# A four-branch encoder layer on one core: q and k by rows of three parts in DRAM, gating on chip, a third tile bank, the norm in 13 steps

## The chip, the cores and the metric
The kernel runs on one core of one Trainium2 chip. A core has TensorE (PE, matmuls into PSUM), VectorE (DVE), ScalarE (ACT) and GpSimd (POOL), and SyncE (SP), which here issues nearly all DMAs. Each engine works through its own instructions in order and waits on semaphores where a tile isn't ready. The metric is device time in microseconds, the median of several executions.

## What is computed
One layer on 1024 tokens with 1024 channels, all in float32:

```python
h = rmsnorm(x, norm_g[l])
z = h @ w_in[l]
qa, ka, va, glu_a, glu_b, pool_in, sgu_u, sgu_v, gates = jnp.split(z, split_at, axis=-1)
y_a = neighborhood_attention(qa, ka, va, na_rpb[l])
y_b = conformer_conv(glu_a, glu_b, conv_dw_w[l], conv_dw_b[l], conv_ln_g[l], conv_ln_b[l], conv_pw[l])
y_c = multiscale_pool(pool_in, pool_w[l], pool_scale[l])
y_d = spatial_gating(jax.nn.gelu(sgu_u), jax.nn.gelu(sgu_v), sgu_ln_g[l], sgu_ln_b[l], sgu_w[l], sgu_b[l])
y = jnp.concatenate([y_a, y_b, y_c, y_d], axis=-1) * jax.nn.silu(gates)
x = x + y @ w_out[l]
```

A last rmsnorm follows. Attention has 8 heads of 32 channels over windows of 8 x 16 tokens. The convolution branch is a depthwise convolution of 31 taps, a LayerNorm over its 256 channels (mean and variance over channels, so over partitions here), a swish and a 256 x 256 matmul. The spatial gating multiplies u by a mix of v over 128 positions.

## The kernel before
Matmuls take float32 split into a high and a low part, three products each (hi x hi, hi x lo, lo x hi).

**Column tiles.** `w_in` is worked through in 20 column tiles of 128 channels by 1024 tokens. `prep` loads a tile's weights (wraw) and splits them (whi, wlo). `gemm_bank` makes one half of a tile, 512 tokens, in one PSUM bank z_ps by 24 matmuls (L371), and an `evac_*` function takes it out. I number these 40 halves banks 0 to 39. The order of tiles is the list `work`: GLU gates and values (GB0, GA0, GB1, GA1), Q0, K0, pool (PO0, PO1), u (U0, U1), Q1, K1, and then the eight gate tiles G6, G7, G4, G5, G0, G2, G3, G1 (banks 24 to 39). Two PSUM banks are shared by all z_ps; the convolution has its own accumulator bank (ac), small matmuls another (b_ps), attention outputs another (pv), and scores two tiles (sa, sb).

**Work beside the column tiles.** After each bank the main loop takes pieces from three generators: attention (18 steps over banks 18 to 37), the convolution's 97 taps (over banks 4 to 22; most are DVE instructions, L584) and the convolution's norm (5 steps over banks 23 to 27). So the program's order is set by this count; a scheduler then places the instructions on each engine. Attention step j makes the scores of two heads for 256 queries (`att_scores`, L475 to L478, eight small matmuls), the exponent of step j-1 (`att_exp`, DVE L481 to L509 and ACT L500; M is a maximum, R a sum, rp on POOL a reduction over partitions) and, every second step, an output (`att_out`, L516 and L520). Steps 0 to 7 are head group 0 and 8 to 15 head group 1.

**Keys and queries.** `evac_q` and `evac_k` write hi and lo of a head group to DRAM (q_d, k_d, 128 partitions). `att_keys` loads a head's key tile kst: three loads of 32 partitions (hi, lo, hi) and one of 32 constant rows (kc_d). `att_loads` does the same for the queries (qst) and loads vk. All are issued on SP, in order.

**The norm.** `conv_norm` subtracts the mean (L612 makes it, L614 subtracts it), makes the variance (L622), sends it through DRAM in two hops (s_d, cr, sq) to spread it over partitions, scales (L637), applies the swish (L641 to L644) and makes the 256 x 256 matmul in yb (L651, L652).

**The gates.** `evac_u` makes u and, with `sgu` results, the gated u; it stores it to yd_d in DRAM. `evac_g` multiplies a branch by its gate: for tiles 6, 7 (spatial gating) and 4, 5 (pool) it loads the branch from DRAM into yr at its first half (L722), takes tanh (L725), multiplies z by yr (L727) and adds (L728). L730 and L731 do the same for branches that are in SBUF. After bank 39 the output GEMM begins (L822 on).

## Time and profile before
| | us |
|---|---|
| median of 3 runs | 436.57 (436.07 to 437.01) |
| the profiled execution | 435.86 |
| its span in the trace | 434.1 |
| PE busy | 415.9 (96%) |
| DVE busy | 312.3 (72%) |
| ACT busy | 184.8 (43%) |
| POOL busy | 112.2 (26%) |

PE is the engine that sets the time; its granted clock is at full speed but for one dip. A share of busy time is an average over the whole span: what a change is worth is read in the stretch where it acts, from the windows, the waits and the timeline of that stretch. A row of the timeline gives the start, the time from the first start to the last end of equal neighbours, the engine, the line, output <- input, the shape and the count, and in brackets the idle time before it with what ended it. Matmuls overlap, so the pitch from start to start tells more than the length of one.

### The profile page before, as it was taken

What the parts mean: (1) busy time and instruction counts of PE and PEld (TensorE: products, weight loads), DVE (VectorE), ACT (ScalarE), POOL (GpSimd) and SP (SyncE); (2) the same over time, 40 slices, a digit from 0 to 9 for tenths busy, and PEclk for the clock granted to TensorE, in tenths of its full rate; (3) what the DMA queues carried; (4) which work ended last, traced back from release to release, by engine and by line L of the source; (5) the groups of instructions that cost most, each with busy time, mean ns of one, the idle gap of its engine ahead of it and who ended that gap; (6) DMA issues with size and microseconds to landing.
All of it is one profiled execution on the core that took longest, in us unless ns stands there. A gap on an engine that the chain in (4) does not pass through costs nothing.

```text
span 434.1 us, 5888 instructions
## 1 busy us (share of the span) xinstructions
PE 415.9 (96%) x2150; PEld 331.2 (76%) x2150; DVE 312.3 (72%) x540; ACT 184.8 (43%) x314; POOL 112.2 (26%) x90
## 2 busy tenths in 40 slices
PE   7899999999999999999978889999999999999994
PEld 6788878888888778777846647787787788888883
DVE  4798676888988799999798647997882580093332
ACT  6757655222232328334336733344342452254332
POOL 0763402322226821111111101221111243620000
PEclk9999999999999999999995999999999999999998
DMA  7995106311775124163893141522011384402222
GB/s 273 421 418 186 54 25 206 88 48 51 228 245 150 48 97 146 50 219 104 271 235 90 52 168 54 170 94 65 11 48 61 122 269 183 145 2 97 97 98 97
DMA packets 28294, 59.56 MB, mean 137 GB/s; under 512 B 3910, under 2 KB 13354, under 8 KB 28266
## 3 DMA queue, kind: packets, MB, share of 16 engines
q1 hardware_dynamic: 28122, 58.93, 40.9%
q8 instruction: 17, 0.28, 0.3%
q10 hardware_dynamic: 144, 0.26, 0.2%
q14 instruction: 11, 0.09, 0.1%
HBM read 46.71 MB, written 12.47 MB: 136 GB/s over the span
## 4 chain that ended last, share of the span: by engine, by line
PE 80%; DMA 9%; DVE 5%; SPq 2%; ACT 1%; issue 1%; POOL 1%; DVEq 0%; ACTq 0%; POOLq 0%
PE z_ps L371 45%; DMA yr<-yd_d 3%; PE sb L213 3%; PE z_ps L213 3%; PE sb L822 3%; PE sb L856 3%; PE z_ps L822 2%; PE b_ps L856 2%; PE z_ps L856 2%; DMA xT_sb<-in_xT_dram 2%; PE pv L516 2%; PE sa L822 1%; PE ac L213 1%; PE b_ps L822 1%; PE pv L822 1%; PE ac L822 1%
## 5 line engine op out<-in xcount | busy, mean ns | idle before, releaser
L371 PE MATMUL z_ps<-hhi,whi 128*128 128x512 f32 x320 | 90.0, 400 | 1.5 <-DVE yr L728 1.3
L371 PE MATMUL z_ps<-hlo,whi 128*128 128x512 f32 x320 | 89.6, 398 | 0.0
L371 PE MATMUL z_ps<-hhi,wlo 128*128 128x512 f32 x320 | 87.8, 395 | 0.0
L371 PEld LDWEIGHTS z_ps<-hhi,whi 128*128 128x128 f32 x320 | 59.3, 190 | 17.8 <-issue 3.0
L371 PEld LDWEIGHTS z_ps<-hlo,whi 128*128 128x128 f32 x320 | 60.3, 189 | 14.8 <-issue 2.5
L371 PEld LDWEIGHTS z_ps<-hhi,wlo 128*128 128x128 f32 x320 | 60.5, 190 | 13.8 <-issue 1.1
L488 POOL PARTITION_ALL_REDUCE R<-M x16 | 29.9, 1868 | 134.3 <-DVE M L509 128.9
L584 DVE SCALAR_TENSOR_TENSOR ac<-d,pk,ac 128x512 f32<-128x512 f32 x62 | 46.6, 751 | 2.6 <-ACT ac L596 0.9
L360 POOL TENSOR_TENSOR wlo<-wraw,whi 128x256 fp32r<-128x256 f32 x36 | 27.4, 784 | 68.6 <-ACT whi L354 68.6
L354 ACT ACTIVATE whi<-wraw 128x512 fp32r<-128x512 f32 x40 | 25.0, 627 | 33.3 <-PE z_ps L371 31.5
L500 ACT ACTIVATE T<-T 128x1280 f32<-128x1280 f32 x16 | 20.4, 1272 | 15.5 <-DVE T L499 15.5
L584 DVE SCALAR_TENSOR_TENSOR ac<-ch,dws,ac 128x512 f32<-128x512 f32 x30 | 22.6, 755 | 1.8 <-ACT ac L585 0.8
L831 ACT ACTIVATE jk<-res 128x512 f32<-128x512 f32 (+1 forms) x17 | 10.2, 604 | 26.6 <-DVE res L829 25.6
L356 DVE TENSOR_TENSOR wlo<-wraw,whi 128x512 fp32r<-128x512 f32 x22 | 16.8, 764 | 5.1 <-ACT whi L354 5.0
L781 POOL TENSOR_TENSOR wlo<-wraw,whi 128x512 fp32r<-128x512 f32 x8 | 12.1, 1524 | 31.7 <-ACT whi L780 18.9
L829 DVE SCALAR_TENSOR_TENSOR res<-sa,res 128x512 f32<-128x512 f32 x2 | 1.4, 686 | 22.6 <-PE sa L822 22.6
L725 ACT ACTIVATE sg<-z_ps 128x512 f32<-128x512 f32 x16 | 9.5, 596 | 15.5 <-PE z_ps L371 14.1
L499 DVE TENSOR_TENSOR T<-T,pv 128x768 f32<-128x768 f32 x16 | 15.2, 948 | 0.0
L483 DVE SCALAR_TENSOR_TENSOR T<-sb,bt 128x768 f32<-128x768 f32 x16 | 15.2, 948 | 0.0
L505 DVE TENSOR_TENSOR R<-T 128x512 f32<-128x512 f32 x16 | 13.2, 827 | 2.6 <-ACT T L500 2.6
L481 DVE SCALAR_TENSOR_TENSOR T<-sa,bt 128x512 f32<-128x512 f32 x16 | 11.0, 685 | 3.7 <-PE pv L516 2.4
L781 POOL TENSOR_TENSOR wl<-wraw,wh 128x512 fp32r<-128x512 f32 x8 | 10.2, 1294 | 11.3 <-ACT wh L780 11.3
(279 smaller groups left out, 821.6 us busy)
## 6 DMA issues: line engine op xcount, KB each, us to landing
wraw<-in_w_in_dram SPq DMA_DIRECT2D x20, 512.0 KB
res<-in_x_dram SPq DMA_DIRECT2D x8, 512.0 KB
wraw<-in_w_out_dram SPq DMA_DIRECT2D x8, 512.0 KB
out_dram<-res SPq DMA_DIRECT2D x15, 256.0 KB
kst<-k_d SPq DMA_DIRECT2D x24, 136.0 KB
xT_sb<-in_xT_dram SPq DMA_DIRECT2D x6, 512.0 KB
qst<-q_d SPq DMA_DIRECT2D x24, 128.0 KB
vk<-va_d SPq DMA_DIRECT2D x8, 256.0 KB
```

The lines of the kernel that those rows point to most:

```text
L213: pe.matmul(z, lhsT=ha[:, 2 * c + k, ts], rhs=wa[:, k, :], start=(c == 0 and n == 0 and k == 0), stop=(c == 3 and n == 2 and k == 1))
L354: s.activation(out=hi, in_=raw[:, 4 * q:4 * q + 4], func=AF.Copy)
L356: v.tensor_tensor(out=lo, in0=raw[:, 4 * q:4 * q + 4], in1=hi, op=ALU.subtract)
L360: g.tensor_tensor(out=lo[:, w:w + 2], in0=raw[:, 4 * q + w:4 * q + w + 2], in1=hi[:, w:w + 2], op=ALU.subtract)
L371: pe.matmul(z, lhsT=wa[:, k, :], rhs=ha[:, 4 * q + k, b * 512:(b + 1) * 512], start=(n == 0), stop=(n == 3 * KO - 1))
L483: v.scalar_tensor_tensor(out=T[:, :, 256:640], in0=sb[:, :, 0:384], scalar=DH ** -0.5, in1=mf, op0=ALU.mult, op1=ALU.add)
L488: g.partition_all_reduce(R.rearrange("p h x -> p (h x)"), M.rearrange("p h x -> p (h x)"), P, bass.bass_isa.ReduceOp.max)
L500: s.activation(out=T, in_=T, func=AF.Exp)
L584: v.scalar_tensor_tensor(out=ac, in0=src, scalar=w, in1=ac, op0=ALU.mult, op1=ALU.add)
L781: g.tensor_tensor(out=lo[q], in0=raw[:, q], in1=hi[q], op=ALU.subtract)
L822: pe.matmul(acc[t], lhsT=y_[kt][:, ts], rhs=w_[q], start=(j == 0 and q == 0 and n == 0), stop=(j == 3 and q == 1 and n == 2))
L856: pe.matmul(o[:, c0:c1], lhsT=y_[kt][:, ts], rhs=w_[j][:, q, c0:c1], start=(j == 0 and q == 0 and n == 0), stop=(j == 3 and q == 1 and n = ...
```

## The change
Four parts.

- q_d and k_d hold, for each of 128 channels, a row of three parts (hi, hi, lo for q and hi, lo, hi for k). Three stores in place of two for each; a key tile is loaded by one DMA of 96 partitions, queries by one too. The key tiles are four fixed buffers (kst0 to kst3), so the constant rows are loaded for head group 0 only.
- The gated u stays in its SBUF tile (ut) and is tile 6 and 7's branch; yd_d, its two stores and two loads are gone. The pool branch's loads (yc_d) are issued two tiles ahead (`back`).
- Of the gate tiles' banks 24, 27, 30 and 33 go into the convolution's accumulator bank (ac), which gives three banks in turn.
- The convolution ends at bank 21, and the norm has 13 steps over banks 22 to 33 in place of 5 over 23 to 27. yb uses the tiles of sq.

```diff
-ATT0, ATT1, CONV0, CONV1 = 18, 37, 4, 22
+ATT0, ATT1, CONV0, CONV1, NORM1 = 18, 37, 4, 21, 33
...
     ya += [slot("ya") for _ in range(2)]
-    yr = {kt: slot("yr") for kt in (6, 7, 4, 5)}
+    yr = {kt: slot("yr") for kt in (4, 5)}
     sq = [slot("sq") for _ in range(2)]
-    yb = [slot("yb") for _ in range(2)]
+    yb = sq
 
...
-        z = zbank()
+
+        z = pso.tile([P, 512], F32, name="ac") if CONV1 < bank < ATT1 - 1 and bank % 3 == 0 else zbank()
...
-    k_d = dram.tile([2, 2, 4, DH, SW], F32, name="k_d")
+
+    q_d = dram.tile([2, P, 3, S], F32, name="q_d")
+    k_d = dram.tile([2, P, 3, SW], F32, name="k_d")
...
-                for n, src in enumerate((hi, lo)):
-                    ld.dma_start(out=q_d[hg, n].rearrange("h d x -> (h d) x"), in_=src[:, 0:S].bitcast(F32))
+                for n, src in enumerate((hi, hi, lo)):
+                    ld.dma_start(out=q_d[hg, :, n], in_=src[:, 0:S].bitcast(F32))
...
-                for n, src in enumerate((hi, lo)):
-                    ld.dma_start(out=k_d[hg, n].rearrange("h d x -> (h d) x"), in_=src.bitcast(F32))
+                for n, src in enumerate((hi, lo, hi)):
+                    ld.dma_start(out=k_d[hg, :, n], in_=src.bitcast(F32))
...
 
+
+    kbuf = {}
+
+    def ktile(h):
+        if h not in kbuf:
+            kbuf[h] = at.tile([P, SW], F32R, name=f"kst{h}", bufs=1)
+        return kbuf[h]
+
     def att_loads(gi):
         hg, b = groups[gi]
         vk[gi] = at.tile([P, 4, P], F32, name="vk")
@@ -433,20 +443,18 @@
                                              ap=[[GW, P], [256 * GW, 4], [1, P]]))
         qst[gi] = at.tile([P, 4, 256], F32R, name="qst")
 
-        for n in range(2):
-            src = q_d[hg, n, :, :, b * 256:(b + 1) * 256]
-            for c in range(2 - n):
-                o = 64 * n + 32 * c
-                ld.dma_start(out=qst[gi][o:o + 32].bitcast(F32), in_=src.rearrange("h d x -> d h x"))
+        src = q_d[hg, 0:DH, 0, b * 256:(b + 1) * 256]
+        ld.dma_start(out=qst[gi][0:96].bitcast(F32),
+                     in_=bass.AP(tensor=src.tensor, offset=src.offset, ap=[[S, 96], [96 * S, 4], [1, 256]]))
         ld.dma_start(out=qst[gi][96:128].rearrange("p h x -> p (h x)").bitcast(F32), in_=qm_d[32 * b:32 * b + 32])
 
     def att_keys(hg, h):
-        kst[hg, h] = at.tile([P, SW], F32R, name="kst", bufs=4)
-
-
-        for c, n in enumerate((0, 1, 0)):
-            ld.dma_start(out=kst[hg, h][32 * c:32 * c + 32].bitcast(F32), in_=k_d[hg, n, h])
-        ld.dma_start(out=kst[hg, h][96:128].bitcast(F32), in_=kc_d)
+
+        kst[hg, h] = ktile(h)
+        ld.dma_start(out=kst[hg, h][0:96].bitcast(F32),
+                     in_=k_d[hg, DH * h:DH * h + DH].rearrange("d n x -> (d n) x"))
+        if hg == 0:
+            ld.dma_start(out=kst[hg, h][96:128].bitcast(F32), in_=kc_d)
 
...
+            yield
...
+        yield
         for c in range(2):
             v.tensor_tensor(out=cc[c][:, 0:S], in0=cc[c][:, 0:S], in1=rb, op=ALU.mult)
+            s.activation(out=cc[c][:, 0:S], in_=cc[c][:, 0:S], func=AF.Identity, scale=cvec[:, 1, c:c + 1],
+                         bias=cvec[:, 2, c:c + 1])
+            yield
 
         for c in range(2):
             t = sq[c][:, 0:S]
-            s.activation(out=cc[c][:, 0:S], in_=cc[c][:, 0:S], func=AF.Identity, scale=cvec[:, 1, c:c + 1],
-                         bias=cvec[:, 2, c:c + 1])
             s.activation(out=t, in_=cc[c][:, 0:S], func=AF.Tanh, scale=0.5)
             v.scalar_tensor_tensor(out=cc[c][:, 0:S], in0=t, scalar=1.0, in1=cc[c][:, 0:S], op0=ALU.add, op1=ALU.mult)
-        yield
+            yield
         for c in range(2):
             for b in range(2):
-                sl = slice(b * 512, (b + 1) * 512)
                 ps = bbank()
                 for k in range(2):
-                    pe.matmul(ps, lhsT=pw[:, k, c * P:(c + 1) * P], rhs=cc[k][:, sl], start=(k == 0), stop=(k == 1))
+                    pe.matmul(ps, lhsT=pw[:, k, c * P:(c + 1) * P], rhs=cc[k][:, b * 512:(b + 1) * 512], start=(k == 0),
+                              stop=(k == 1))
                 s.activation(out=yb[c][:, 0:S].rearrange("p (n e) -> p n e", e=2)[:, :, b], in_=ps, func=AF.Copy, scale=0.5)
-            yield
-
-
-    yd_d = dram.tile([2, P, S], F32, name="yd_d")
+                yield
+
 
     def evac_u(c):
...
-            if b == 1:
-                ld.dma_start(out=yd_d[c], in_=u[:, 0:S])
...
 
-    y = {0: ya[0], 1: ya[1], 2: yb[0], 3: yb[1]}
+    y = {0: ya[0], 1: ya[1], 2: yb[0], 3: yb[1], 6: ut[0], 7: ut[1]}
     y.update(yr)
 
-    def evac_g(kt, src):
+    def evac_g(kt, early):
         def f(b, z):
             br = y[kt]
             sl = slice(b * 512, (b + 1) * 512)
-            if b == 0 and src is not None:
-                ld.dma_start(out=br[:, 0:S], in_=src)
 
             sg = at.tile([P, 512], F32, name="sg")
             s.activation(out=sg, in_=z, func=AF.Tanh, scale=0.5)
-            if src is not None:
...
-    work += [(T_G + kt, evac_g(kt, src)) for kt, src in
-             ((6, yd_d[0]), (7, yd_d[1]), (4, yc_d[0]), (5, yc_d[1]), (0, None), (2, None), (3, None), (1, None))]
+    work += [(T_G + kt, evac_g(kt, n < 4)) for n, kt in enumerate((6, 7, 4, 5, 0, 2, 3, 1))]
+
+    back = {T_G + kt: (yr[kt], yc_d[kt - 4]) for kt in (4, 5)}
 
...
+        if n + 2 < len(work) and work[n + 2][0] in back:
+            dst, src = back[work[n + 2][0]]
+            ld.dma_start(out=dst[:, 0:S], in_=src)
 
         for b in ((1, 0) if n == 0 else (0, 1)):
             evac(b, gemm_bank(ct, b))
             bank += 1
             if bank == 2:
                 bias_rows()
...
                 if b0 <= bank:
                     for _ in range(done(bank, count, b0, b1) - done(bank - 1, count, b0, b1)):
```

What that does to the instructions' order, at three places. Lines of after are 1 to 11 higher: L372 is the column-tile matmul, L483 to L486 the scores, L524 and L528 the output, L732/L733 and L735/L736 the gates' products.

SP, before, the loads for head group 1 (key tiles by parts of 32 partitions, then queries, then the spatial gating's load):

```order
L526 DMA o_d<-sg 4x256
L448 DMA kst<-k_d 32x1088 x4
L449 DMA kst<-kc_d 32x1088
L349 DMA wraw<-in_w_in_dram 128x1024
L448 DMA kst<-k_d 32x1088 x3
L449 DMA kst<-kc_d 32x1088
L448 DMA kst<-k_d 32x1088 x3
L449 DMA kst<-kc_d 32x1088
L440 DMA qst<-q_d 32x4x256 x3
L441 DMA qst<-qm_d 32x1024
L432 DMA vk<-va_d 128x4x128
L722 DMA yr<-yd_d 128x1024
```

SP, after, the same place:

```order
L534 DMA o_d<-sg 4x256
L454 DMA kst_1428<-k_d 96x1088
L454 DMA kst_1431<-k_d 96x1088
L759 DMA yr<-yc_d 128x1024 x2
L349 DMA wraw<-in_w_in_dram 128x1024
L454 DMA kst_1511<-k_d 96x1088
L454 DMA kst_1514<-k_d 96x1088
L447 DMA qst<-q_d 96x4x256
L449 DMA qst<-qm_d 32x1024
L635 DMA s_d<-sg 4x256
```

The four key tiles are four DMAs in place of sixteen, and the two pool loads (yc_d) stand ahead of the last two key tiles and the queries; the yd_d load is gone.

PE, before, between bank 25 and bank 26 (L622 is the variance, L475 to L478 scores, both steps 8 and 9 together):

```order
L622 MATMUL b_ps<-sq,mean_w 32x256 x4
L475 MATMUL sa<-qst,kst 128x128
L476 MATMUL sa<-qst,kst 128x128
L475 MATMUL sa<-qst,kst 128x128
L476 MATMUL sa<-qst,kst 128x128
L477 MATMUL sb<-qst,kst 128x192
L478 MATMUL sb<-qst,kst 128x192
L477 MATMUL sb<-qst,kst 128x192
L478 MATMUL sb<-qst,kst 128x192
L371 MATMUL z_ps<-hhi,whi 128x512 x4
L371 MATMUL z_ps<-hhi,wlo 128x512 x4
L371 MATMUL z_ps<-hlo,whi 128x512 x4
```

PE, after, the end of bank 26, the output of group 3 and the start of bank 27:

```order
L372 MATMUL z_ps<-hlo,whi 128x512
L372 MATMUL z_ps<-hhi,whi 128x512 x4
L372 MATMUL z_ps<-hhi,wlo 128x512 x2
L631 MATMUL b_ps<-sq,mean_w 32x256 x4
L372 MATMUL z_ps<-hhi,wlo 128x512 x2
L372 MATMUL z_ps<-hlo,whi 128x512 x2
L524 MATMUL pv<-T,vk 32x128 x2
L372 MATMUL z_ps<-hlo,whi 128x512 x2
L524 MATMUL pv<-T,vk 32x128 x6
L524 MATMUL pv<-T,vk 32x192 x8
L528 MATMUL pv<-R,ones 32x256 x4
L372 MATMUL ac<-hhi,whi 128x512 x4
```

The variance (L631) and the output stand among column-tile matmuls, and bank 27 is in ac; in before two score blocks and the variance stood in a row with no column tile between them.

PE, before, from the last scores of step 14 (L477, L478) to the first of step 15:

```order
L477 MATMUL sb<-qst,kst 128x192
L478 MATMUL sb<-qst,kst 128x192
L371 MATMUL z_ps<-hhi,wlo 128x512 x2
L371 MATMUL z_ps<-hlo,whi 128x512 x4
L371 MATMUL z_ps<-hhi,whi 128x512 x4
L371 MATMUL z_ps<-hhi,wlo 128x512 x4
L371 MATMUL z_ps<-hlo,whi 128x512 x4
L371 MATMUL z_ps<-hhi,whi 128x512 x4
L371 MATMUL z_ps<-hhi,wlo 128x512 x4
L371 MATMUL z_ps<-hlo,whi 128x512 x4
L475 MATMUL sa<-qst,kst 128x128
L476 MATMUL sa<-qst,kst 128x128
```

PE, after, from bank 35 (it stands between the two halves of step 15's scores) to group 6's output (L524, L528):

```order
L372 MATMUL z_ps<-hhi,wlo 128x512 x4
L372 MATMUL z_ps<-hlo,whi 128x512 x4
L372 MATMUL z_ps<-hhi,whi 128x512 x4
L372 MATMUL z_ps<-hhi,wlo 128x512 x4
L372 MATMUL z_ps<-hlo,whi 128x512 x4
L485 MATMUL sb<-qst,kst_1511 128x192
L486 MATMUL sb<-qst,kst_1511 128x192
L485 MATMUL sb<-qst,kst_1514 128x192
L486 MATMUL sb<-qst,kst_1514 128x192
L524 MATMUL pv<-T,vk 32x128 x8
L524 MATMUL pv<-T,vk 32x192 x8
L528 MATMUL pv<-R,ones 32x256 x4
```

Before, 30 matmuls of L371 lie between the scores of steps 14 and 15 and 10 more between step 15's and group 6's output; after, the 24 of bank 35 are all that lies between step 14's scores and that output.

DVE, after, the rows ahead of the R of step 13 (the last L517 of this piece), which that output needs:

```order
L736 TENSOR_TENSOR ya<-sg,ya 128x512
L513 TENSOR_TENSOR R<-T 128x512
L736 TENSOR_TENSOR ya<-sg,ya 128x512
L517 TENSOR_TENSOR R<-R,T 128x2x128
L356 TENSOR_TENSOR wlo<-wraw,whi 128x512
L513 TENSOR_TENSOR M<-T 128x512
L505 TENSOR_TENSOR T<-T,pv 128x2x256
L507 TENSOR_TENSOR T<-T,pv 128x2x384
L517 TENSOR_TENSOR M<-M,T 128x2x128
L356 TENSOR_TENSOR wlo<-wraw,whi 128x512
L513 TENSOR_TENSOR R<-T 128x512
L517 TENSOR_TENSOR R<-R,T 128x2x128
```

DVE, before, the rows ahead of the same R (the last L509):

```order
L483 SCALAR_TENSOR_TENSOR T<-sb,bt 128x2x384
L505 TENSOR_TENSOR R<-T 128x512
L497 TENSOR_TENSOR T<-T,pv 128x2x256
L499 TENSOR_TENSOR T<-T,pv 128x2x384
L730 SCALAR_TENSOR_TENSOR sg<-sg,z_ps 128x512
L505 TENSOR_TENSOR M<-T 128x512
L356 TENSOR_TENSOR wlo<-wraw,whi 128x512
L509 TENSOR_TENSOR R<-R,T 128x2x128
L731 TENSOR_TENSOR ya<-sg,ya 128x512
L509 TENSOR_TENSOR M<-M,T 128x2x128
L505 TENSOR_TENSOR R<-T 128x512
L509 TENSOR_TENSOR R<-R,T 128x2x128
```

Counted from the first DVE row that reads step 14's scores (L489 after, L481 before) to this R there are 20 rows after and 13 before; among the 20 are the gate products of two banks.

## Rows read from the trace of the kernel before
**Rows 1.** The page: busy time of the engines.

```profile
PE 415.9 (96%) x2150; PEld 331.2 (76%) x2150; DVE 312.3 (72%) x540; ACT 184.8 (43%) x314; POOL 112.2 (26%) x90
```

**Rows 2.** Windows: length, busy us (PE, PEld, DVE, ACT, POOL), clock, DMA share, GB/s.

```profile
175.00:200.00 25.00, 25.00 (x173) 19.50 (x172) 25.00 (x44) 8.33 (x14) 3.83 (x2) 1.00 0.34 117
...
204.67:256.12 51.45, 44.26 (x239) 30.03 (x237) 39.90 (x62) 24.39 (x35) 7.67 (x4) 0.90 0.57 166
...
204.67:226.34 21.67, 18.80 (x118) 13.51 (x116) 19.47 (x32) 8.20 (x12) 4.10 (x2) 1.00 0.85 247
226.34:236.58 10.24, 8.79 (x31) 6.54 (x32) 9.14 (x15) 5.50 (x9) 1.78 (x1) 0.50 0.49 130
236.58:256.12 19.54, 16.67 (x92) 9.98 (x90) 11.29 (x16) 10.69 (x15) 1.79 (x1) 1.00 0.29 95
...
204.67:323.90 119.23, 111.70 (x640) 82.97 (x639) 97.07 (x150) 52.02 (x77) 20.42 (x11) 0.96 0.39 116
```

**Rows 3.** Timeline of PE around 300 to 328 us.

```profile
298.88 0.23 PE L475 MATMUL sa<-qst,kst 128*128 128x128 f32 x1
...
299.75 0.65 PE L371 MATMUL z_ps<-hhi,wlo 128*128 128x512 f32 x2
...
320.81 1.07 PE L371 MATMUL z_ps<-hhi,whi 128*128 128x512 f32 x4
...
326.34 1.29 PE L516 MATMUL pv<-T,vk 128*32 128x128 f32 x32
...
328.00 0.50 PE L822 MATMUL sa<-whi,yhi 128*128 128x512 f32 x1
```

**Rows 4.** Timeline of PE, 225 to 256 us.

```profile
225.56 0.33 PE L475 MATMUL sa<-qst,kst 128*128 128x128 f32 x1
...
232.06 2.07 PE L371 MATMUL z_ps<-hhi,whi 128*128 128x512 f32 x4 [1.32 <-DVE yr L728]
...
251.34 1.98 PE L651 MATMUL b_ps<-cc,pk 128*128 128x512 f32 x4 [0.71 <-ACT yb L652]
```

**Rows 5.** PE's waits over the span: us in total, times, longest.

```profile
PE pv L520 <- DVE R L509: 1.8, 2, 1.4
PE b_ps L651 <- ACT yb L652: 1.4, 2, 0.7
PE b_ps L651 <- DVE cc L644: 1.4, 2, 0.8
PE z_ps L371 <- DVE yr L728: 1.3, 1, 1.3
```

**Rows 6.** Chain of waits, 200 to 300 us: start, length, piece.

```profile
224.21 6.28 DMA yr<-yd_d
...
249.20 4.95 DMA yr<-yd_d
```

**Rows 7.** Timeline of DVE at the two L727 and around 305 us.

```profile
230.59 0.70 DVE L727 TENSOR_TENSOR z_ps<-z_ps,yr 128x512 f32<-128x512 f32 x1 [0.74 <-DMA yr<-yd_d]
...
254.18 1.30 DVE L727 TENSOR_TENSOR z_ps<-z_ps,yr 128x512 f32<-128x512 f32 x2 [4.13 <-DMA yr<-yd_d]
...
303.33 0.68 DVE L497 TENSOR_TENSOR T<-T,pv 128x512 f32<-128x512 f32 x1
303.93 0.95 DVE L499 TENSOR_TENSOR T<-T,pv 128x768 f32<-128x768 f32 x1
304.80 0.68 DVE L730 SCALAR_TENSOR_TENSOR sg<-sg,z_ps 128x512 f32<-128x512 f32 x1
...
306.60 0.42 DVE L509 TENSOR_TENSOR R<-R,T 128x256 f32<-128x256 f32 x1
306.93 0.69 DVE L731 TENSOR_TENSOR ya<-sg,ya 128x512 f32<-128x512 f32 x1
...
308.59 1.14 DVE L509 TENSOR_TENSOR R<-R,T 128x256 f32<-128x256 f32 x1
```

**Rows 8.** DMA rate, 120 to 140 us by half microseconds: k_d stores, then key loads.

```profile
GB/s 0 0 0 164 344 410 262 426 418 418 418 409 113 253 261 279 287 244 261 209 253 253 244 235 235 235 225 225 222 319 433 339 87 26 49 0 0 0 0 0
```

More of the change, by code (lines that the diff above doesn't have):

```diff
@@ L374, in gemm_bank @@
         return z
-    q_d = dram.tile([2, 2, 4, DH, S], F32, name="q_d")
-    k_d = dram.tile([2, 2, 4, DH, SW], F32, name="k_d")
+    q_d = dram.tile([2, P, 3, S], F32, name="q_d")
+    k_d = dram.tile([2, P, 3, SW], F32, name="k_d")
     o_d = dram.tile([2, 4, 4, 256], F32, name="o_d")
@@ L720, in f @@
             sl = slice(b * 512, (b + 1) * 512)
-            if b == 0 and src is not None:
-                ld.dma_start(out=br[:, 0:S], in_=src)
             sg = at.tile([P, 512], F32, name="sg")
             s.activation(out=sg, in_=z, func=AF.Tanh, scale=0.5)
-            if src is not None:
+            if early:
                 v.tensor_tensor(out=z, in0=z, in1=br[:, sl], op=ALU.mult)
@@ L756, in encoder_kernel @@
                 bias_rows()
-            for gen, count, b0, b1 in ((att, 18, ATT0, ATT1), (conv, 97, CONV0, CONV1), (norm, 5, CONV1 + 1, CONV1 + 5)):
+            for gen, count, b0, b1 in ((att, 18, ATT0, ATT1), (conv, 97, CONV0, CONV1), (norm, 13, CONV1 + 1, NORM1)):
                 if b0 <= bank:
```

## The prediction, made before the change was run

> **What bounds the kernel now.** I read the page first: TensorE (PE) is busy 96% of the span [rows 1], so a gain must come out of the few places where it stands or runs slowly. The windows show where those are. [...] So 7.2 us are idle, and of the 8.79 busy us at half clock half, 4.4 us, are lost: 11.6 us.
>
> The same loss from the other side, by durations. A bank takes 5.53 us (320.81 to 326.34), a score block 0.87 (298.88 to 299.75), an attention output 1.66 (326.34 to 328.00) [rows 3]. The stretch holds 4 banks (22.1), 4 score blocks (3.5), two outputs and the tail of a third (3.7), three fours of L651 at 1.98 (5.9) [rows 4], four matmuls of L612 of the same shape (2.0) and eight small ones of L622 (0.5, by the eight of a score block). That is 37.7, so 13.7 us are lost. The two counts bracket the pot: **11.6 to 13.7 us, I take 12.6**.
>
> Who causes it: the list of PE's waits has R from L509 (1.8 us, two times), the convolution's chain L644 and L652 ahead of L651 (1.4 each), and yr from L728 (1.3) [rows 5]. The chain of waits names what lies behind: 6.28 and 4.95 us for yr<-yd_d, the spatial gating result that was sent to DRAM and is fetched back [rows 6]. On DVE L727 stands for that load, 0.74 us at 230.59 and 4.13 us at 254.18, and everything behind it in DVE's order stands too [rows 7]. PE's fall to half clock follows a stretch in which it stood 2.9 us (18.80 busy of 21.67, nearly all at its end).
>
> **The change, part by part.**
> *Spatial gating stays on chip.* Two stores and two loads of 512 KB go. L732 (L727 of before) now finds its operand in SBUF, so the chain pieces of 6.28 and 4.95 us and DVE's 0.74 and 4.13 us end [rows 6, 7]. What is late next there is DVE's own queue: the 0.60 us product waits in order behind score and exponent work, not behind a DMA. The two yc_d loads now stand two tiles earlier, ahead of the last two key buffers and of qst on SP. Moved there they cost DMA time: 1.0 MB at the 235 to 250 GB/s that key loads of before show [rows 8] is 4.2 to 4.5 us. Cover: the scores of step 8, the first of head group 1, began at 225.56 [rows 4]. In the order of after, three banks and 20 matmuls of a fourth, two outputs, two score blocks, L620 and L631 lie between 204.67 and them, 16.6 + 4.6 + 3.3 + 1.7 + 2.0 + 0.5 = 28.7 us, so PE gets there near 233.4, 8 us later. The third rival is the case in which that cover is gone.
>
> *q and k in DRAM by rows of three parts.* Per head group one more store of 512 and one of 544 KB: at 418 GB/s, which stores reach from 128 partitions [rows 8], 1.2 and 1.3 us. Against it go, for head group 1, the four constant rows (4 x 136 KB, 2.3 us at 235 GB/s) and the yd_d stores, and 24 key and 24 query issues become 8 and 8. Loads of 96 partitions are not in the trace; they lie between the loads of 32 (235 to 250 GB/s) and the stores of 128 (418), so four of 408 KB take 4.0 to 7.1 us where twelve of 136 KB took 6.7 to 7.1. Net of this part and the last, those keys and queries land between 0 and 4 us later than in before. Under 8 us of cover that is zero on the path. The rows show narrow transfers slower than wide ones. [...]
>
> *Third bank for column tiles.* Banks 24, 27, 30 and 33 use the convolution's accumulator, free since the convolution now ends at bank 21 (97 taps in 18 banks and not 19; DVE held 25.00 of 25 us there, so its queue is no lighter, but PE held too). It removes the wait for a z bank whose product DVE has not finished (1.3 us at 232.06) [rows 4, 5].
>
> *The norm in 13 steps over banks 22 to 33.* L651's eight pairs no longer stand in one block, where PE waited 1.4 us for L644 and 1.4 for L652 [rows 5], but between column-tile matmuls. These 2.8 us are in the pot. The instructions are the same, so ACT and DVE get no new work; yb in sq's tiles adds a wait for the reader of the tanh, which is 2 steps old by then, so nothing.
>
> *What DVE gives back.* Without stalls PE catches up with DVE. DVE is busy 97.07 of 119.23 us from 204.67 to 323.90 [rows 2]; with 12.6 us less it needs 91%, against 100% held in 175 to 200. Its order decides where it bites: in after there is between the scores of step 14 and the output of group 6 less PE work than before. Before: R of step 13 was done 10.85 us after PE began those scores (298.88 to 308.59 + 1.14) [rows 3, 7] and PE had 40 column-tile matmuls and the scores of step 15 to do meanwhile. After: 0.87 for the scores, half a score block (0.43), one bank (5.53), the other half (0.44) and the output's L524 (1.1): 8.4 us. At the same pace PE stands **2.4 us**. If instead DVE is just in step with the scores, its 20 rows up to that R are 13 at a pitch of 0.60, 3 at 0.87 and 4 at 0.33 [rows 7], 11.7 us, against 6.4 us of PE work: 5.3 us. Then bank 36 waits for L735 of bank 34, four rows further (0.60 + 0.87 + 0.60 + 0.60 = 2.7) while PE has the output's 1.66: **1.0 us** more. Bounds 0 (DVE runs ahead) to 6.3; I take 2.4 + 1.0 = 3.4, as the row of before is the nearest.
>
> **Sum.** 434.1 - 12.6 + 3.4 = 424.9 us of span. The profiled execution took 435.86, 1.76 more than its span, and lies 0.71 under the median of 436.57: 424.9 + 1.76 + 0.71 = **427.4 us**. Its own bounds: pot 13.7 and no stall 422.9; pot 11.6 and 6.3 us of stall 431.3.
>
> **The rivals.**
> *1, the clock falls again.* For: in before the clock fell after PE had stood 2.9 us; a stall of 3 to 6 us near 300 us is of that kind. Against: from 236.58 to 256.12 it stood 2.9 us too, spread between the L651 pairs, and the clock stayed at 1.00 [rows 2]. The fall would cost 4.4 us as in before, and the stall up to 2.9 more than I take: 427.4 + 4.4 = 431.8 to 434.7.
>
> *2, all stalls go.* DVE runs ahead because L732 never waits: 423, or some 421 where the gaps after bank 28 shrink too.
>
> *3, slower: the keys of head group 1 come late.* SP issues in order, and yc_d (1.0 MB) and the third stores stand ahead of the last keys and of qst. If the 96-partition loads ran at half the 235 GB/s, the 1.7 MB would take 14.2 us in place of 7.1; with the 4 us from above that is 11 us, 3 beyond the cover. Then the LayerNorm's s_d and cr transfers, behind qst on SP, are late too, and L638 waits for them on DVE with the products of banks 25 to 27 behind it: another bank's time, up to 5.5 us. With a half-clock stretch of 4.4: 427.4 + 3 + 5.5 + 4.4 = 440.3. Slower than before it is from 10 us of these 13 on, that is from loads at some 120 GB/s down. Against: no load of before is that slow.
>
> *4, the change moves the stalls and doesn't end them.* DVE's late products are replaced by its late R over the whole stretch; the idle 7.2 us return and the clock dips once: 427.4 + 7.2 = 434.6 to 437.
>
> **How the numbers follow.** Chances: forecast 0.50, rival 1 0.22, rival 2 0.10, rival 3 0.11, rival 4 0.07 (0.06 of it within 0.2%, the rest slower). A measurement of this kernel tells about 0.2% (0.9 us) from no change, so faster means under 435.7 and slower above 437.4. The forecast and rivals 1 and 2 lie below: 0.82; same 0.06; slower 0.11 + 0.01 = 0.12. For 8 in 10 the range goes from rival 2 to the top of rival 1: 421 to 434.7.
>
> **What would show it.** Right: no yr<-yd_d anywhere, L732 without a DMA as releaser, PE busy without a break and at clock 1.00 from 200 to 256, bank 28 beginning near 234 to 240 in place of 256.12, L661 without waits over 0.3 us; PE waiting for R of L517 or for L735 shortly after 295 us, by 2 to 6 us; conv ending about one bank earlier. Wrong: PE waiting for a kst or qst load at step 8 of the scores (rival 3); a half-clock slice near 300 (rival 1); DVE under 85% busy with PE still idle, which would mean that the order, not DVE's load, makes the stalls. The forecast fails if PE's idle time after 200 us stays above 7 us or if the clock dips more than once.

## The result and the profile after

The changed kernel takes 431.28 us (430.8 to 431.84, 4 runs) where before takes 436.32 in the same runs: a ratio of 0.9884, 95% interval 0.9865 to 0.9904, faster by 5.0 us. The forecast was 427.4, inside its range of 421 to 434.7, and the time of the first rival was 431.8 to 434.7. The profiled execution took 431.34, its span is 429.5.

The page of after: its span, the busy times, and the chain that ended last by engine. It answers to [rows 1].

```profile
span 429.5 us, 5815 instructions
PE 414.4 (96%) x2150; PEld 331.4 (77%) x2150; DVE 309.4 (72%) x540; ACT 185.1 (43%) x314; POOL 112.5 (26%) x90
...
PE 83%; DVE 7%; DMA 5%; ACT 1%; SPq 1%; issue 1%; POOL 1%; DVEq 0%; ACTq 0%; POOLq 0%
```

The shares of busy time say nothing new; the stretches do. Windows of before, then of after (length, busy us of PE, PEld, DVE, ACT, POOL, clock, DMA share, GB/s):

```profile
200.00:250.00 50.00, 44.33 (x288) 31.92 (x287) 42.58 (x67) 25.29 (x36) 9.72 (x5) 0.90 0.58 165
250.00:290.00 40.00, 38.13 (x197) 27.77 (x196) 30.74 (x49) 16.03 (x24) 5.35 (x3) 1.00 0.39 130
290.00:340.00 50.00, 50.00 (x320) 39.33 (x319) 32.77 (x54) 16.30 (x28) 8.68 (x5) 1.00 0.16 49
```

```profile
200.00:250.00 50.00, 49.62 (x333) 36.89 (x332) 40.29 (x63) 24.62 (x36) 9.88 (x5) 1.00 0.60 184
250.00:290.00 40.00, 39.82 (x206) 29.57 (x204) 32.44 (x50) 16.35 (x26) 7.68 (x4) 1.00 0.26 81
290.00:340.00 50.00, 43.72 (x276) 33.83 (x276) 34.53 (x51) 19.39 (x31) 9.52 (x6) 0.90 0.18 56
```

The idle time and the half clock of 200 to 290 us [rows 2] are gone, and 6.3 idle us and a half-clock stretch stand between 290 and 340, where before had none. Bank 28 begins at 234.9 in place of 256.12, 21 us earlier, which is not all gain: group 4's output and the norm's matmuls (L651 of before) stood ahead of bank 28 and now stand behind it. Bank 36 at 309.91 in place of 315.37, 5.5 us earlier; the last half of the output GEMM at 379.43 in place of 383.81. TensorE's waits, as in [rows 5] (us in total, times, longest):

```profile
PE pv L524 <- issue: 2.5, 1, 2.5
PE z_ps L372 <- DVE sg L735: 2.5, 2, 2.0
...
PE pv L524 <- ACT T L508: 0.6, 1, 0.6
```

And PE's timeline in after, the start of bank 28 and then the waits of that stretch:

```profile
234.90 1.20 PE L372 MATMUL z_ps<-hhi,whi 128*128 128x512 f32 x4 [0.38 <-DVE u L733]
...
292.13 0.33 PE L483 MATMUL sa<-qst,kst 128*128 128x128 f32 x1 [0.35 <-DVE T L489]
...
293.09 0.33 PE L485 MATMUL sb<-qst,kst 128*128 128x192 f32 x1 [0.29 <-DVE T L491]
...
294.79 1.19 PE L372 MATMUL z_ps<-hhi,whi 128*128 128x512 f32 x4 [0.54 <-DVE sg L735]
...
303.48 0.64 PE L524 MATMUL pv<-T,vk 128*32 128x128 f32 x4 [2.52 <-issue]
304.74 2.03 PE L524 MATMUL pv<-T,vk 128*32 128x128 f32 x26 [0.61 <-ACT T L508]
...
309.91 2.08 PE L372 MATMUL z_ps<-hhi,whi 128*128 128x512 f32 x4 [1.97 <-DVE sg L735]
...
317.16 1.07 PE L372 MATMUL z_ps<-hhi,whi 128*128 128x512 f32 x4
```

The six waits from 292 us on (all but that of bank 28) add up to 6.28 us. The first L524 at 303.48 is group 6's output. The profile names no releaser for its 2.52 us ("issue"); what ends just before it is DVE's L507 of step 13, which reads the one bank pv that this output writes. The next wait ends with step 13's exponent on ACT:

```profile
302.44 0.94 DVE L507 TENSOR_TENSOR T<-T,pv 128x768 f32<-128x768 f32 x1
...
303.41 1.27 ACT L508 ACTIVATE T<-T 128x1280 f32<-128x1280 f32 x1 [2.21 <-DVE T L507]
```

So the output waits where the prediction had it, for step 13, which is late on DVE; but the listed waits are for pv and the exponent, not for the sums R that the prediction named. Bank 36 waits for L735 of bank 34, as the prediction had it. From 303.29 the granted clock is 0.50 for 10.24 us, of which PE is busy 7.47 (a window of after):

```profile
303.29:313.53 10.24, 7.47 (x49) 5.08 (x50) 9.08 (x16) 5.27 (x8) 3.84 (x2) 0.50 0.10 38
```

That stretch runs into bank 36: the bank takes 7.25 us, from 309.91 to 317.16.

DVE at the beginning of that stretch, in after (timeline):

```profile
291.38 0.69 DVE L489 SCALAR_TENSOR_TENSOR T<-sa,bt 128x512 f32<-128x512 f32 x1 [3.18 <-PE pv L524]
...
292.86 0.68 DVE L489 SCALAR_TENSOR_TENSOR T<-sa,bt 128x512 f32<-128x512 f32 x1
```

DVE stood 3.18 us before 291.38, because the next score tile T is one that group 5's output on PE still read, and PE came to that output only after bank 34. Then PE and DVE met: DVE reads the first half of step 14's scores at 292.86, and PE makes their second half from 293.09, so DVE is in step with PE and not ahead.

### The profile page after: what moved, and what is told of

Read it like the earlier page. It is cut to its first block, busy times and chain, and to the rows that moved or that the text cites. A ratio compares the mean times of both kernels' runs of the same rounds, so it can differ in the third digit from the quotient of the medians.

```text
span 429.5 us, 5815 instructions
## 1 busy us (share of the span) xinstructions
PE 414.4 (96%) x2150; PEld 331.4 (77%) x2150; DVE 309.4 (72%) x540; ACT 185.1 (43%) x314; POOL 112.5 (26%) x90
## 4 chain that ended last, share of the span: by engine, by line
PE 83%; DVE 7%; DMA 5%; ACT 1%; SPq 1%; issue 1%; POOL 1%; DVEq 0%; ACTq 0%; POOLq 0%
PE z_ps L372 42%; PE ac L372 3%; PE sb L213 3%; PE z_ps L213 3%; PE sb L865 3%; PE z_ps L831 3%; PE sb L831 3%; PE pv L524 2%; PE b_ps L865 2%; PE z_ps L865 2%; DMA xT_sb<-in_xT_dram 2%; DMA wraw<-in_w_in_dram 1%; DMA s_d<-sg 1%; PE ac L213 1%; PE pv L865 1%; PE ac L865 1%
## 5 line engine op out<-in xcount | busy, mean ns | idle before, releaser
L372 PE MATMUL z_ps<-hhi,whi 128*128 128x512 f32 x288 | 80.7, 400 | 2.9 <-DVE sg L735 2.5
L372 PE MATMUL z_ps<-hlo,whi 128*128 128x512 f32 x288 | 81.7, 399 | 0.0
L372 PE MATMUL z_ps<-hhi,wlo 128*128 128x512 f32 x288 | 78.6, 394 | 0.0
L372 PEld LDWEIGHTS z_ps<-hhi,whi 128*128 128x128 f32 x288 | 53.8, 190 | 17.1 <-DVE sg L735 3.5
L496 POOL PARTITION_ALL_REDUCE R<-M x16 | 31.5, 1968 | 127.8 <-DVE M L517 89.0
L372 PEld LDWEIGHTS z_ps<-hlo,whi 128*128 128x128 f32 x288 | 53.8, 188 | 13.8 <-issue 3.1
L372 PEld LDWEIGHTS z_ps<-hhi,wlo 128*128 128x128 f32 x288 | 54.4, 190 | 12.3 <-issue 0.8
L790 POOL TENSOR_TENSOR wlo<-wraw,whi 128x512 fp32r<-128x512 f32 x8 | 11.0, 1379 | 35.3 <-ACT whi L789 35.3
L524 PE MATMUL pv<-T,vk 128*32 128x128 f32 (+1 forms) x256 | 14.8, 325 | 3.1 <-issue 2.5
L489 DVE SCALAR_TENSOR_TENSOR T<-sa,bt 128x512 f32<-128x512 f32 x16 | 11.0, 685 | 8.3 <-PE pv L524 8.0
L524 PEld LDWEIGHTS pv<-T,vk 128*32 128x32 f32 x256 | 8.4, 116 | 9.8 <-issue 6.7
L513 DVE TENSOR_TENSOR R<-T 128x512 f32<-128x512 f32 x16 | 12.9, 803 | 4.3 <-ACT T L508 4.3
L491 DVE SCALAR_TENSOR_TENSOR T<-sb,bt 128x768 f32<-128x768 f32 x16 | 15.2, 947 | 0.0
L507 DVE TENSOR_TENSOR T<-T,pv 128x768 f32<-128x768 f32 x16 | 15.1, 946 | 0.0
```

The costliest lines, as they stand in the source:

```text
L372: pe.matmul(z, lhsT=wa[:, k, :], rhs=ha[:, 4 * q + k, b * 512:(b + 1) * 512], start=(n == 0), stop=(n == 3 * KO - 1))
L491: v.scalar_tensor_tensor(out=T[:, :, 256:640], in0=sb[:, :, 0:384], scalar=DH ** -0.5, in1=mf, op0=ALU.mult, op1=ALU.add)
L496: g.partition_all_reduce(R.rearrange("p h x -> p (h x)"), M.rearrange("p h x -> p (h x)"), P, bass.bass_isa.ReduceOp.max)
L524: pe.matmul(pv[32 * h:32 * h + 32, o0:o0 + c1 - c0], lhsT=vk[gi][:, kt, 32 * h:32 * h + 32], rhs=pts[2 * gi + h // 2][0][:, h % 2, c0:c1], ...
```

## The experiments

**Each part taken back.** Four kernels are the changed one without one of its parts.

```diff
-        z = pso.tile([P, 512], F32, name="ac") if CONV1 < bank < ATT1 - 1 and bank % 3 == 0 else zbank()
+        z = zbank()
```

> The changed kernel with two z banks only, as before (parts 1, 2 and 4 kept). Theory A, that the late stall comes from DVE's order and load and that the third bank spares TensorE a wait for a z bank in banks 24 to 30: the wait of L372 for L733 comes back for 1 to 3 us between 218 and 256 us, the late stall shrinks by about as much, 431 to 433 us. Rival, that the third bank lets TensorE run ahead and so makes the late stall near 300 us: no stall and no half clock there, 426 to 429 us.

Measured 443.06 us, ratio 1.0156 (1.0133 to 1.018): 11.8 us slower than the changed kernel and slower than before. Neither theory had that. Windows of this run:

```profile
200.00:250.00 50.00, 42.51 (x256) 31.15 (x256) 39.01 (x61) 23.39 (x34) 11.59 (x5) 0.90 0.56 173
250.00:290.00 40.00, 35.60 (x212) 25.37 (x210) 26.22 (x42) 13.84 (x23) 5.62 (x3) 0.94 0.27 80
290.00:340.00 50.00, 48.03 (x298) 37.56 (x299) 34.57 (x54) 18.35 (x29) 8.67 (x5) 0.94 0.12 39
```

7.5, 4.4 and 2.0 us of idle PE and two half-clock stretches. The first begins on DVE (timeline of DVE, then of PE):

```profile
231.54 0.17 DVE L638 TENSOR_SCALAR cr<-cr 128x8 f32<-128x8 f32 x1 [4.24 <-DMA cr<-s_d]
...
234.44 0.70 DVE L732 TENSOR_TENSOR z_ps<-z_ps,u 128x512 f32<-128x512 f32 x1 [2.25 <-ACT sg L730]
```

```profile
235.79 0.48 PE L483 MATMUL sa<-qst,kst 128*128 128x128 f32 x1 [4.06 <-DVE T L489]
```

DVE stands 4.24 us for the load of the LayerNorm's variance (cr), with the products that free the next bank (L732, then L733) behind it in order, and PE then stands 4.06 us for a score that DVE has not read. In the changed kernel the same L638 waits 0.23 us: there the third bank's products (L732 at 225.12, L733 at 225.85), then a step's scores (L489 at 227.35, L491 at 227.96) and the next L732 stand on DVE ahead of it while the transfer runs (timeline of DVE, after):

```profile
231.36 0.70 DVE L732 TENSOR_TENSOR z_ps<-z_ps,u 128x512 f32<-128x512 f32 x1 [1.66 <-ACT sg L730]
232.28 0.17 DVE L638 TENSOR_SCALAR cr<-cr 128x8 f32<-128x8 f32 x1 [0.23 <-DMA cr<-s_d]
```

With two banks that step's scores had come at 224.51, and after 227.31 nothing stands ahead of L638. The load is not later here: L638 begins at 231.54, 0.74 us earlier than in the changed kernel.

```diff
-ATT0, ATT1, CONV0, CONV1, NORM1 = 18, 37, 4, 21, 33
+ATT0, ATT1, CONV0, CONV1, NORM1 = 18, 37, 4, 22, 27
...
-(norm, 13, CONV1 + 1, NORM1)
+(norm, 5, CONV1 + 1, NORM1)
```

with `conv_norm` as in the kernel before.

> The changed kernel with the convolution to bank 22 and its norm in 5 steps over banks 23 to 27, as before (parts 1 to 3 kept). Theory A, that the block of the convolution's 256 x 256 matmuls costs TensorE its 2.8 us of waits and the gain of spreading is of that size: the waits of L651's successor for the cc product and the yb copy come back, 433 to 435 us. Rival, that the DVE and ACT work of the norm only changes place and the late stall takes up the difference: within 1 us of 431.3.

Measured 438.01 us, ratio 1.0038 (1.0019 to 1.0057): 6.7 us slower than the changed kernel. The direction is theory A's, the size over twice the 2.8 us of waits; and the waits that theory A names, ahead of the convolution's 256 x 256 matmuls, are not in this run's list. Bank 27 begins at 233.53 in place of 227.87, with a half-clock stretch of 6.83 us from 231.89, and the late waits near 310 us stay (the longest 3.1 us ahead of group 6's output). Ahead of that half clock DVE stands for the norm's means (L620), whose second half PE makes at 224.70 (timeline of DVE):

```profile
225.86 1.29 DVE L622 TENSOR_TENSOR cc<-cc,b_ps 128x512 f32<-128x512 f32 x2 [2.08 <-PE b_ps L620]
```

The changed kernel has no wait of DVE over 1.1 us between 218 and 229. That this wait carries the 6.7 us is read from the order, not shown by a run.

```diff
+            if b == 1:
+                ld.dma_start(out=yd_d[c], in_=u[:, 0:S])
...
+            if b == 0 and kt in src_d:
+                ld.dma_start(out=br[:, 0:S], in_=src_d[kt])
```

> The changed kernel with the gated u stored to DRAM and loaded again at its tile's first half, as before (parts 1, 3 and 4 kept). Theory A, that the wait of DVE for yr<-yd_d carried most of the idle time and the half clock of 218 to 256 us: that wait returns with 4 us or more, TensorE stands 4 to 8 us there, 434 to 438 us. Rival, that the queue of 24 key and 24 query issues carried it: with parts 1, 3 and 4 in place the load lands in time, 431 to 432 us.

Measured 432.89 us, ratio 0.9925 (0.9901 to 0.995): only 1.6 us slower. Theory A is refuted for this place. In this kernel SP issues the two yr<-yd_d loads at 217.29 and 218.41 (they were at 224.21 and 249.20 in before [rows 6]), ahead of the last two key tiles, the queries and vk; no wait of DVE for yd_d is left. What made the pieces of 6.28 and 4.95 us was the place of the load in SP's order, not the trip through DRAM. This run also shows a late cr<-s_d that costs DVE little. SP issues it at 233.65 (230.72 in the changed kernel), and DVE has a gate product ahead of its reader (timeline of DVE):

```profile
234.28 0.70 DVE L738 TENSOR_TENSOR z_ps<-z_ps,yr 128x512 f32<-128x512 f32 x1 [1.97 <-ACT sg L736]
...
236.12 0.17 DVE L638 TENSOR_SCALAR cr<-cr 128x8 f32<-128x8 f32 x1 [0.55 <-DMA cr<-s_d]
```

```diff
-        ld.dma_start(out=kst[hg, h][0:96].bitcast(F32),
-                     in_=k_d[hg, DH * h:DH * h + DH].rearrange("d n x -> (d n) x"))
+        for c, n in enumerate((0, 1, 0)):
+            ld.dma_start(out=kst[hg, h][32 * c:32 * c + 32].bitcast(F32), in_=k_d[hg, n, h])
```

and the same for the queries and the stores.

> The changed kernel with q and k in DRAM as before and their loads of 32 partitions (parts 2 to 4 kept). Theory A, that these loads are covered by TensorE's work either way: within 1 us of 431.3, with key loads at 235 to 250 GB/s and no wait of TensorE for kst or qst over 1 us. Rival, that the loads of 96 partitions are what makes step 8 of the scores come in time: TensorE or DVE wait 3 us or more there, 434 to 438 us.

Measured 439.32 us (ten runs from 434.81 to 441.27), ratio 1.0056 (1.0027 to 1.0085): 8 us slower than the changed kernel. PE waited for no kst or qst, so the loads themselves are not late. DVE, then SP, in this run (timeline):

```profile
233.72 0.17 DVE L632 TENSOR_SCALAR cr<-cr 128x8 f32<-128x8 f32 x1 [4.83 <-DMA cr<-s_d]
...
234.41 0.69 DVE L726 TENSOR_TENSOR z_ps<-z_ps,u 128x512 f32<-128x512 f32 x1
```

```profile
225.35 0.51 SPq L629 DMA_DIRECT2D s_d<-sg  x1
229.69 0.30 SPq L450 DMA_DIRECT2D kst<-k_d  x1
230.03 0.42 SPq L451 DMA_DIRECT2D kst<-kc_d  x1
230.66 0.32 SPq L442 DMA_DIRECT2D qst<-q_d  x1
231.13 0.34 SPq L631 DMA_DIRECT2D cr<-s_d  x1
```

The small transfer cr<-s_d is issued among the last key and query loads, at 231.13 against 230.72 in the changed kernel, and its reader begins 1.44 us later than there (233.72 against 232.28). The rest of the 4.83 us is DVE's order: L726, the product of bank 25, stands behind the reader here and ahead of it in the changed kernel (L732 at 231.36). That bank is the one that bank 28 is to use, so PE waits 3.10 us at 237.61 for bank 28. It is the second half of the prediction's third rival, in the kernel with the old loads. Bank 28 begins at 237.61 in place of 234.9; further waits of 1.4 and 2.84 us follow near 285.

**One or two parts alone**, on the kernel before.

```diff
-    yr = {kt: slot("yr") for kt in (6, 7, 4, 5)}
+    yr = {kt: slot("yr") for kt in (4, 5)}
...
-    y = {0: ya[0], 1: ya[1], 2: yb[0], 3: yb[1]}
+    y = {0: ya[0], 1: ya[1], 2: yb[0], 3: yb[1], 6: ut[0], 7: ut[1]}
```

> The kernel before with the gated u kept on chip alone (no yd_d; the pool branch's loads stay where they were). Theory of the prediction, that DVE's wait for yr<-yd_d is what makes the pieces of 6.28 and 4.95 us in the chain of waits: 427 to 432 us. Rival, after the run in which the trip through DRAM was put back and cost only 1.6 us, that this load was late because it stood behind the key and query loads on SP, and that with it gone DVE stands for cr<-s_d behind the same queue: 434 to 437 us.

Measured 432.59 us, ratio 0.9922 (0.9905 to 0.9939): faster by 3.4 us, two thirds of the whole change. Its windows:

```profile
200.00:250.00 50.00, 45.33 (x300) 33.36 (x299) 44.41 (x70) 25.93 (x38) 9.73 (x5) 0.93 0.52 151
250.00:290.00 40.00, 39.48 (x234) 28.80 (x233) 31.13 (x51) 15.24 (x23) 7.14 (x4) 1.00 0.34 107
290.00:340.00 50.00, 48.93 (x284) 39.02 (x283) 31.82 (x49) 16.95 (x29) 8.64 (x5) 1.00 0.15 49
```

Idle time of 250 to 290 falls from 1.87 to 0.52 us and the half-clock stretch from 10.24 to 6.83 us; 4.67 us of 200 to 250 stay idle. No wait of DVE for the cr load is in its list.

The rows of three parts alone (the diff's part on q_d, k_d, qst and kst, nothing else):

> The kernel before with q and k in DRAM by rows of three parts and their loads of 96 partitions alone. Theory of the prediction, that these loads are covered: 435.5 to 437.5 us. Rival, that the queue on SP is what makes the waits between 218 and 256 us: the yr<-yd_d load is issued and lands 3 us or more earlier, and 430 to 434 us.

Measured 435.83 us, ratio 1.0001 (0.999 to 1.0012): no difference. Alone, the loads are covered as the prediction had it, and L733 there still waits 4.6 us for yr<-yd_d, which SP issues at 223.93 and 250.31 (before: 224.21 and 249.20): its place in SP's order sets it, not the length of the loads ahead. It stands right behind vk<-va_d (223.50), which SP holds for 4.0 us until PE's output (L526).

```diff
-        z = zbank()
+        z = pso.tile([P, 512], F32, name="ac") if CONV1 < bank < ATT1 - 1 and bank % 3 == 0 else zbank()
```

on top of e_gate_alone:

> The kernel before with the gated u on chip and the third bank for column tiles (parts 2 and 3; loads of q and k and the norm as before). The third bank was worth 11.8 us on top of the other three parts. Theory C, that it is what lets TensorE go on while DVE's queue is held at the convolution's cr: it shortens the wait before bank 26 too, 425 to 430 us. Rival, that it was worth so much only because the norm's spread-out steps stand in DVE's queue at that place: within 1.5 us of the 432.6 of e_gate_alone.

Measured 433.73 us, ratio 0.9956 (0.9924 to 0.9988): no gain over e_gate_alone. The rival's time holds: beside the gate alone the third bank is worth nothing, in the changed kernel 11.8 us. Whether it needs the spread norm, the new loads or both was not tried.

**The late stall.** Two kernels fill the gap ahead of group 6's output with matmuls whose result is not used, and leave the order of PE ahead of that output as it was (behind it, the last output comes later among the column tiles).

```diff
+            if j == n - 1:
+                ps = bbank()
+                for k in range(7):
+                    pe.matmul(ps, lhsT=ones, rhs=pts[n - 4][1].rearrange("p h x -> p (h x)"), start=(k == 0), stop=(k == 6))
```

> The changed kernel with seven matmuls more (the sum R of step 12 by ones, into the free b_ps bank, result unused) just ahead of group 6's output, where TensorE stood from 300.97 to 303.48 us; the order of all else is the same. By the durations of L661 they fill some 3 us of that gap. Theory A, that the stall is DVE's and the clock falls because TensorE stood: the output begins at about the same time (within 0.5 us), the clock stays at 1.00 near 303 us, and of the 7.47 us busy at half clock 3.7 are saved: 427.5 to 428.5 us. Rival, that the clock falls for the whole sparse stretch from 290 us on, whatever fills this one gap: the half clock stays and the time is 431 to 432 us.

Measured 433.78 us, ratio 0.9946 (0.9926 to 0.9966). The seven became 14 records and 6.25 us, twice what I had counted, so the output began at 307.43. The clock stayed at 1.00 from there to 426 us. So neither theory came out whole: there is no half clock, and the kernel is 2.5 us slower than the changed one. But this run has bank 36 at full clock, 5.57 us from its start to bank 37's (PE's timeline):

```profile
311.76 1.19 PE L372 MATMUL z_ps<-hhi,whi 128*128 128x512 f32 x4 [2.61 <-DVE sg L739]
...
317.33 1.07 PE L372 MATMUL z_ps<-hhi,whi 128*128 128x512 f32 x4
```

With three of these matmuls:

> As e_fill, with three of these matmuls in place of seven (14 records at a pitch of 0.45 us in e_fill, so six here, 2.7 us, which fit the gap from 300.97 to 303.48). Theory A, that the clock fell in the changed kernel because TensorE stood in that gap, and that e_fill lost what it won by filling 3 us too long: the output of group 6 begins within 0.5 us of 303.9, no half clock near 303 us, bank 36 begins at 306.5 to 308.5 in place of 309.91, 428 to 429.5 us. Rival, that the clock was not the cause of the loss: 431 to 432 us with the clock at 1.00.

Measured 430.99 us, ratio 0.9879 (0.9837 to 0.9921): as the changed kernel. PE's timeline of this run:

```profile
300.80 2.81 PE L556 MATMUL b_ps<-R,ones 128*128 128x512 f32 x6
303.55 0.41 PE L524 MATMUL pv<-T,vk 128*32 128x128 f32 x4
...
309.08 1.19 PE L372 MATMUL z_ps<-hhi,whi 128*128 128x512 f32 x4 [2.14 <-DVE sg L739]
...
316.27 1.07 PE L372 MATMUL z_ps<-hhi,whi 128*128 128x512 f32 x4
```

The half clock of 303 us is gone (one of 3.41 us comes at 310.16, after PE stood 2.14 us). The output begins within 0.1 us of the changed kernel's, and bank 36 only 0.83 us earlier, since it waits for DVE's L739 (L735 of after) in any case. So the half clock ahead of bank 36 costs 0.8 us: while PE waits for DVE, it loses little by being slow. That is the rival's reading, for this part. The part on bank 36 itself, where PE sets the pace, is in this run as in the changed kernel: the bank takes 7.19 us here and 7.25 there, against 5.57 at full clock in e_fill. That is another 1.7 us, so I estimate the whole half-clock stretch of the changed kernel at 2.5 us from these three runs. Of the 0.9 us that bank 37 begins earlier here, 0.7 go again where the output GEMM (L835) waits for L739, so the time of this run doesn't show them.

A fourth score tile T, with one slot fewer in the shared pool to pay for it:

```diff
-NSLOT = 10
+NSLOT = 9
...
-        T = at.tile([P, 2, 640], F32, name="T", bufs=3)
+        T = at.tile([P, 2, 640], F32, name="T", bufs=4)
```

> The changed kernel with four score tiles T in place of three (one slot fewer of the shared pool pays for the space). Theory A1, that the late stall begins with DVE's wait for a T that group 5's output on TensorE still reads (3.18 us before 291.38 us in the changed kernel): that wait goes, the late stall shrinks by 3 us or more, and without the half clock 422 to 428 us. Rival A2, that DVE's load in that stretch sets it: DVE's idle time only moves, 430 to 433 us.

Measured 454.67 us, ratio 1.0429 (1.0395 to 1.0463). The test says nothing of T: DVE's waits for T held by L524 fall from 8.0 to 4.1 us, but the missing slot costs far more, above all in the output GEMM, where DVE now waits 5.8 us for a residual load and PE runs at half clock from 438.62 to the end. What T alone does stays open.

```diff
-ATT0, ATT1, CONV0, CONV1, NORM1 = 18, 37, 4, 21, 33
+ATT0, ATT1, CONV0, CONV1, NORM1 = 18, 38, 4, 21, 33
```

> The changed kernel with the attention's 18 steps spread over banks 18 to 38 in place of 37. DVE has one bank more for the same work, and the scores of step 14 and the output of group 6 lie further apart. Theory A, that the late stall is a matter of how densely the last steps stand: TensorE's waits after 285 us fall from 6.3 to under 3 us, no half clock there, 424 to 429 us. Rival, that the end of attention is on the path then (the last sum, o_d, r_d and the gate of tile 1 come 5 us later): 431 to 436 us with TensorE waiting after 325 us.

Measured 436.15 us, ratio 0.9996 (0.9981 to 1.0012). Both theories are right in part. The late stall is gone: bank 36 begins at 299.32 in place of 309.91 and bank 37 at 304.81 in place of 317.16. But the edit does one thing more: the third bank is given by `bank < ATT1 - 1`, so bank 36 goes into ac here and no longer waits for L735 of bank 34. Which of the two ends the stall, this run doesn't separate. Then the end of attention is on the path (PE, then DVE):

```profile
317.41 0.79 PE L831 MATMUL sa<-wlo,yhi 128*128 128x512 f32 x1 [3.22 <-POOL wlo L790]
...
345.25 0.80 PE L831 MATMUL z_ps<-whi,yhi 128*128 128x512 f32 x1 [5.69 <-DVE sg L735]
```

```profile
342.70 1.29 DVE L547 TENSOR_TENSOR ya<-ya,T 128x512 f32<-128x512 f32 x2 [7.17 <-DMA T<-r_d]
```

L735 of the last bank stands behind L547 on DVE, which waits for a load. The last kernel puts the division by the sums after the gate products:

```diff
-        for k in range(2):
-            rs = slice(8 * k, 8 * k + 8)
+        for rs in (slice(0, 8), slice(8, 16)) if hg == 0 else (slice(0, 16),):
...
     for _ in att:
         pass
+    att_norm(1)
```

> As e_att38, but the division of head group 1's output by its sums (one product in place of two) comes after the gate products of tile 1, with which it commutes; so on DVE the product that frees the last column tile's bank no longer stands behind the load of the sums' reciprocals, for which DVE waited 7.17 us. Theory, that e_att38 had won the late stall (bank 37 began 12.4 us earlier than in the changed kernel) and lost it again at that place: the wait of 5.69 us of L831 for L735 goes, as does the half-clock stretch of 6.83 us behind it, 427 to 431 us. Rival, that the output GEMM then waits for the split of u behind the same load, or for the weights' split on POOL: 433 to 437 us.

Measured 432.74 us, ratio 0.9927 (0.9897 to 0.9956). The 5.69 us wait and the half clock behind it are gone, and 3.4 us are won over e_att38. Waits of 3.8 us for the output weights' split on POOL and 1.7 us for the high part of y on ACT (yhi) are left, and a half-clock stretch from 317 to 325 us behind the first; it stays above the changed kernel. No version here is clearly faster than the changed kernel.

## Why the prediction came out as it did

The measured 431.28 lies in the range, 3.9 us above the forecast, and the forecast's own branch is not what happened: the clock fell near 300 us, which is rival 1.

**The pot** was sized 12.6 us, between 11.6 (idle time and half clock) and 13.7 (durations), and it was emptied: idle time from 200 to 290 us falls from 7.53 to 0.56, at full clock. Bank 28 began at 234.9, inside the 234 to 240 of the forecast. The stretch it was counted in runs from bank 24 to bank 28 of before, the 51.45 us from 204.67 [rows 2]; that half of its 8.79 busy us at a clock of 0.50 are lost is an estimate, and it fits what after shows at that clock, where bank 36's groups of four matmuls start 1.71 us apart (311.78 to 313.49) against 0.91 at 1.00 (315.35 to 316.26). With these 4.4 us of half clock that is 11.4 us, the low end. Another 2.4 us of idle time went outside that stretch, for which the sum had no term: 1.3 ahead of 200 us (one wait of PE for wtm_hi, 0 to 1.3 us among these runs, so not the change's), 0.7 in the output GEMM and 0.4 at the end. With 6.3 us of stall and 2.5 of half clock the account closes to 0.4 us: 434.1 - 11.4 - 2.4 + 6.3 + 2.5 = 429.1, measured 429.5.

**What DVE gives back** is the term that was mis-sized: taken at 3.4 us of 0 to 6.3, it measured 6.28. The place was right. Group 6's output waits 3.1 us (2.52 and 0.61) against 2.4, but for pv and the exponent of step 13 and not for its sums; bank 36 waits 1.97 us for L735 of bank 34 against 1.0. The other 1.2 us are three short waits ahead of bank 35 (0.35, 0.29 and 0.54), for which the sum had no term, so that the whole meets the upper bound of 6.3 is in part luck. I took the low price because the row of before was the nearest; but that row came from an order in which DVE was ahead. In after DVE had stood 3.18 us for a T and was just in step with PE, which is the condition I had named for the high price. The prediction did not look at how many T there are.

**The clock** fell again, rival 1, with 0.22: it fell as PE stood 2.52 us in one piece, at the end of a stretch from 290 us in which PE was busy 9.78 of 13.29 us. Its time of 431.8 to 434.7 lies just above the 431.28 measured. Its price of 4.4 us was too high, since half clock is paid in full only where PE sets the pace: 0.8 us ahead of bank 36 and 1.7 on it, by e_fill3 and e_fill. The sign by which the forecast was to fail, over 7 us of idle PE after 200 us, was met by its words: 12.9 us, of which 6.1 are the kernel's end, after 379.43.

**The parts.** Of q and k I said zero on the path. Alone that is so (435.83 against 435.94 in those runs); taken out of the whole it is 8 us, and the cover did not help, since what DVE waited for was not a key but the small cr<-s_d. The third bank I priced by the one wait of 1.3 us that it removes; it is worth 11.8 us in the whole and nothing beside e_gate_alone. The norm's 2.8 us are 6.7 in the whole, by other waits than the two that I had named. The gate, for which I had the two long chain pieces, is 3.4 us alone and 1.6 in the whole (of its part the gated u alone; the earlier yc_d loads were never taken back). Four parts that add up to 28 us when each is taken out of a change worth 5.0 are not four gains: without the third bank, or without the rows of three parts, DVE stands 4.2 and 4.8 us for the variance and PE behind it, and without the norm's 13 steps 2.1 us for the means; only these three parts together let PE pass the norm. Three parts (q and k, norm, gate) without the third bank are 6.6 us slower than before, while the gate alone has 3.4 of the 5.0.

**Rival 3** did not come (DVE waits 0.2 us for cr in after), but e_qk_old and e_two_banks show its second half, products held behind the wait for cr, with a wait of 4.2 to 4.8 us and a slower kernel than before. I had bound it to slow 96-partition loads and a late transfer. The runs show that what DVE has in its order ahead of the reader decides: with a wait of 4.24 us the reader began at 231.54 (e_two_banks), with one of 0.55 at 236.12 (e_gate_dram). **Rival 4** came in part: 6.28 us of stall stand in place of 7.53 and the clock dips once while PE works, but between 290 and 313 us and not over the whole stretch, and the time stays below its 434.6. **Rival 2** did not come.
